# Second attention: a half head's row sums are turned and stored behind the transposes of its probabilities

## The chip, the cores and the metric

The kernel runs on one core of a Trainium2 chip, as one launch. The metric is the device time of that launch in microseconds (us), the median of several runs. In the profile PE is the matrix engine (PEld its weight loads), DVE the vector engine, ACT the scalar engine, POOL GpSimd, and SP the engine whose queue issues all the DMAs spoken of here.

## The reference

Two layers of an encoder over a prompt of 1024 rows and 8 samples of 16 rows each. Layer 0 has a sliding window with learned sinks; layer 1, the second attention, has chunk-band attention with a bias by clipped distance and no sinks. Cut to what matters here:

```python
s = einsum('bqkgd,bskd->bkgqs', q, k) * ATTN_SCALE + bias
s = where(valid, s, NEG_INF)          # own chunk of 64 and 8 before it
p = softmax(s, axis=-1)               # layer 1: no sinks
o = einsum('bkgqs,bskd->bqkgd', p, v) # 16 heads of 64
x = layer_norm(ALPHA * x + (1 + gate) * (o @ w_o))
```

The kernel doesn't divide the probabilities by their row sums. It multiplies exp(s - m) with the values, and multiplies the result by one over the row sum afterwards. All products are in float32 quality: each operand is split into a high and a low part, and products are summed from them.

## The kernel before

The program is written as one list of calls. A planner then lays the instructions out: it simulates the list, gives each engine a fixed order, and takes among the instructions that it holds to be ready the one that was called earliest. So the place of a call is a rank and not a slot, and each engine then runs its fixed order on the chip and waits where data isn't there.

`attention(l, wk)` runs once for each layer (`l` 0 and 1). The queries of layer 1 are handled as 16 heads (`c` 0 to 7, `a` 0 and 1), each head in two halves of 512 queries (`h` 0 and 1), each half in two pairs of query tiles of 128. `work` holds the 64 pairs and `halves` the 32 halves. The loop over pairs does the following for pair `i`, with `k = i // 2`:

- `scores(x)`: matmuls of scores for two query tiles (lines 558 and 561), and `softmax`: bias and row minimum on DVE (line 525), the exponential with its row sum on ACT (line 529). The row sums go to columns of `L`.
- On every second pair, `sums(halves[k - 1])`: DVE takes one over the 4 columns of row sums of the half that has just been scored (line 633), PE turns them into rows (line 635), DVE copies them out of their PSUM bank to `rl` (line 636), and SP stores them to `rD` in DRAM (line 638).
- By the table `QAT`, the load of a query weight (`qload`) or a third of a head pair's queries (`qblock`, 24 matmuls at line 313, with ACT and DVE at lines 511 and 512).
- On every second pair, `weigh(halves[k - 1])`: PE transposes the half's probabilities in blocks of 128 x 128 (line 587), four to a group and PSUM bank; ACT casts a group to its high part (line 593), and DVE subtracts to get the low part (line 594). A first half (`h` 0) has 10 blocks in 3 groups, a second half 20 blocks in 5.
- With a lag of two pairs, `finish`: `values` multiplies the transposed probabilities with the values (line 609, out by lines 622 and 623), and `normalise` loads the stored row of 1/sum from `rD`, spread over 64 partitions, into `rb` (line 644, SP), multiplies by it on POOL (line 647; the last half on DVE), and stores the result to `oN` (line 649) for `c` under 6 or splits it into the operand of the out-projection. After a second half come the loads of the next head's keys and values (`kload`, lines 488 and 489).
- Behind these, one or more steps of the 16 sample items (lines 683 to 762), which have their own loads (line 689: cached values `cvB`), transposes (727, 749) and matmuls (701, 736). Eight begin from pair 24 on and eight from pair 51 on.

PSUM banks are handed out when the call is made. For transposes there is a ring, `tbk`, which in layer 1 has the three banks 4, 5 and 6 (`TB[1]`). `sums` takes one bank of it, `weigh` one for each group, and a sample item two. Whoever gets a bank waits until it has been emptied by those who had it three takings before.

The last half's `sums` and `weigh` are called behind the loop, in this order.

## Time and profile before

| | |
|---|---|
| runs | 2728.51, 2730.09, 2737.56 us; median 2730.09 |
| profiled execution | 2731.29 us, of which the span is 2729.5 us |
| mean granted PE clock | 0.986 |
| second attention | about 1530 to 1870 us of the span |

A view of the profile is read as follows. A row of the windows view gives start and end of a stretch, its length, then busy us of PE, PEld, DVE, ACT and POOL with their instructions in brackets, the granted PE clock, the busy share of the DMA engines, and GB/s. A row of the waits gives who waited, for whom, the us in total, how often, and the longest. A row of the timeline gives the start in us, the duration in us, the engine, the line, the operation, tiles written and read, the count, and in square brackets how long the engine had been idle and what ended it. A row of the groups gives the line, engine, operation, tiles and shapes, the count, then busy us and the mean ns of one, and last the idle time before them with what ended most of it.

### The profile page before, as it was taken

How to read it: one execution, taken by the hardware profiler on the slowest of the kernel's cores; microseconds unless marked ns; L12 is line 12 of the kernel's file. 1: busy time of each engine (PE TensorE's matmuls, PEld its weight loads, DVE VectorE, ACT ScalarE, POOL GpSimd, SP SyncE). 2: the span in 40 equal slices, each digit the busy share in tenths (PEclk: the TensorE clock that was granted, in tenths of full speed). 3: DMA queues.
4: the chain of work that ended last, by engine and by line, in shares of the span. 5: the costliest groups of instructions: out<-in, count | busy, mean ns of one | idle time of the engine just before them, and what ended most of it. 6: DMA issues, size and time to landing. Idle time of an engine off the chain costs nothing.

```text
span 2729.5 us, 47042 instructions
## 1 busy us (share of the span) xinstructions
PE 2633.3 (96%) x17266; PEld 2342.5 (86%) x17266; DVE 1928.2 (71%) x3840; ACT 1347.8 (49%) x2777; POOL 1069.9 (39%) x771
## 2 busy tenths in 40 slices
PE   7999889999999999999999999989999999999997
PEld 5997768989999998787898888867899999998786
DVE  4376767876677675757764677776878776878668
ACT  3476733543343344444446666672445554546553
POOL 3132523444344347675220121242467666552101
PEclk8999999999999999999999999989999999999999
DMA  8756434644444447666658457784445334349673
GB/s 295 225 158 200 156 104 173 220 172 139 149 150 138 153 138 242 216 227 218 239 191 277 147 151 194 201 243 138 162 149 185 139 126 146 116 145 306 214 237 124
DMA packets 229527, 498.27 MB, mean 183 GB/s; under 512 B 37456, under 2 KB 99232, under 8 KB 229296
## 3 DMA queue, kind: packets, MB, share of 16 engines
q1 hardware_dynamic: 229296, 495.27, 55.0%
q8 instruction: 136, 2.23, 0.3%
q14 instruction: 95, 0.78, 0.1%
HBM read 378.15 MB, written 126.47 MB: 185 GB/s over the span
## 4 chain that ended last, share of the span: by engine, by line
PE 40%; DVE 5%; DMA 2%; ACT 1%; issue 1%; POOL 1%; SPq 0%; DVEq 0%; ACTq 0%; POOLq 0%
PE PS L1237 18%; PE PS L1627 7%; PE PS L326 5%; PE PS L313 4%; PE PS L609 2%; PE PS L587 2%; PE PS L558 1%; PE PS L561 1%; PE PS L736 0%; DMA xa<-actD 0%; DVE F L525 0%; DVE wl L194 0%; DVE xa L194 0%; DMA F<-in_cvB_dram 0%; PE PS L1043 0%
## 5 line engine op out<-in xcount | busy, mean ns | idle before, releaser
L1237 PE MATMUL PS<-H,wh 128*128 128x256 f32 (+1 forms) x2304 | 353.5, 295 | 0.0
L1237 PEld LDWEIGHTS PS<-H,wh 128*128 128x128 f32 x2304 | 320.7, 189 | 0.0
L1197 DVE TENSOR_TENSOR F<-PS,F 128x256 f32<-128x256 f32 (+1 forms) x446 | 197.1, 451 | 162.2 <-PE PS L1237 155.3
L183 ACT CAST wh<-F 128x512 fp32r<-128x512 f32 (+3 forms) x221 | 135.5, 624 | 198.5 <-PE PS L1237 93.8
L194 DVE TENSOR_TENSOR wl<-F,wh 128x512 fp32r<-128x512 f32 (+2 forms) x205 | 193.7, 956 | 45.4 <-ACT wh L183 43.7
L1237 PE MATMUL PS<-H,wl 128*128 128x320 f32 (+1 forms) x1152 | 201.5, 296 | 4.9 <-ACT F L1204 2.5
L1237 PE MATMUL PS<-xa,wh 128*128 128x320 f32 (+1 forms) x1168 | 178.9, 294 | 0.0
L1237 PEld LDWEIGHTS PS<-H,wl 128*128 128x128 f32 x1152 | 169.2, 189 | 10.7 <-issue 4.1
L647 POOL TENSOR_TENSOR F<-F,x2r 64x512 f32<-64x512 f32 x62 | 79.2, 1278 | 213.8 <-DVE F L623 202.0
L1237 PEld LDWEIGHTS PS<-xa,wh 128*128 128x128 f32 x1168 | 162.2, 188 | 0.0
L1495 DVE TENSOR_TENSOR xa<-xa 128x384 fp32r<-128x384 f32 x66 | 100.3, 1531 | 80.2 <-ACT xa L183 78.3
L183 ACT CAST wh<-ws 128x512 fp32r<-128x512 f32 (+1 forms) x123 | 90.8, 745 | 115.8 <-PE PS L1237 51.3
L1357 POOL TENSOR_TENSOR F<-F 128x1152 f32<-128x1152 f32 x44 | 124.7, 2833 | 44.2 <-DVE F L1350 25.1
L313 PE MATMUL PS<-H,w0r 128*128 128x384 f32 (+1 forms) x720 | 137.5, 341 | 0.1
L1286 DVE SCALAR_TENSOR_TENSOR F<-F 128x1024 f32<-128x1024 f32 (+2 forms) x160 | 132.4, 876 | 5.0 <-ACT F L1325 4.1
L326 PE MATMUL PS<-xa,H 128*128 128x512 f32 x504 | 131.0, 401 | 5.0 <-ACT xa L183 3.3
L525 DVE CUSTOM_DVE_ANT_0 F<-PS,F,C 128x256 f32<-128x256 f32 (+3 forms) x208 | 97.2, 479 | 51.6 <-PE PS L561 25.0
L313 PE MATMUL PS<-H,wh 128*128 128x384 f32 (+1 forms) x672 | 132.7, 339 | 0.0
L313 PEld LDWEIGHTS PS<-H,w0r 128*128 128x128 f32 x720 | 125.1, 189 | 1.8 <-DVE F L525 0.4
L587 PE MATMUL PS<-C,F 128*128 128x128 f32 x720 | 112.3, 280 | 7.0 <-DVE C L636 3.1
L326 PEld LDWEIGHTS PS<-xa,H 128*128 128x128 f32 x504 | 95.1, 192 | 27.5 <-ACT xa L183 3.8
L326 PE MATMUL PS<-wh,H 128*128 128x512 f32 (+1 forms) x468 | 117.4, 359 | 0.7 <-ACT wh L183 0.5
(361 smaller groups left out, 6937.7 us busy)
## 6 DMA issues: line engine op xcount, KB each, us to landing
ws<-in_adaw_dram SPq DMA_DIRECT2D x63, 512.0 KB
ws<-in_wup_dram SPq DMA_DIRECT2D x51, 512.0 KB
F<-in_adaw_dram SPq DMA_DIRECT2D x49, 512.0 KB
actD<-F SPq DMA_DIRECT2D x33, 576.0 KB
F<-in_wup_dram SPq DMA_DIRECT2D x37, 512.0 KB
ws<-in_wdn_dram SPq DMA_DIRECT2D x33, 512.0 KB
F<-in_wdn_dram SPq DMA_DIRECT2D x33, 512.0 KB
xa<-kH SPq DMA_DIRECT2D x60, 256.0 KB
```

The source lines that it names most:

```text
L183: nc.scalar.copy(out, in_)
L194: self.eng(el).tensor_sub(lo, src, hi.bitcast(F32))
L313: mm = self.nc.tensor.matmul(out[:, 0:n], w[a][:, k * 128 : k * 128 + 128], H[:, p, k, s0 : s0 + n], start=i == 0, stop=i == 23)
L326: self.nc.tensor.matmul(out[:, 0:n], H[:, p, j * kn + k, t0 : t0 + 128], w[a][:, k * n : k * n + n], start=i == 0, stop=i == 23,)
L525: nc.vector.tensor_tensor_reduce(out=p[:, c0 : c0 + w], in0=ps, in1=b, scale=1.0, scalar=init, op0=ALU.add, op1=ALU.min, accum_out=nm)
L587: nc.tensor.transpose(t[:, n * 128 : n * 128 + 128], p[:, (kt - k0) * 128 : (kt - k0) * 128 + 128], self.ident)
L1197: nc.vector.tensor_add(d, v(ps), a if len(a.shape) == 3 else v(a))
L1237: self.pairmm = nc.tensor.matmul(ps[:, 0:m], w[a][:, k * 128 : k * 128 + 128], x(p, k, n), start=start and c == 0, stop=c == 11, skip_grou ...
L1286: nc.vector.scalar_tensor_tensor(o, u, cw[:, cc, i : i + 1], o, op0=ALU.mult, op1=ALU.add)
L1357: nc.gpsimd.tensor_mul(yg, yg, ya)
L1495: nc.vector.tensor_sub(lo, raw, hi.bitcast(F32))
L1627: self.downmm = nc.tensor.matmul(ps, a[p][:, i * 128 : i * 128 + 128], w[q], start=first and c == 0, stop=last and c == 2, skip_group_chec ...
```

## The change

In layer 1 alone, a half's `sums` is called behind its `weigh`; in layer 0 it stays where it was. The two calls behind the loop, for the last half, are not changed.

```diff
             scores(x)
             k = i // 2
-            if i % 2 == 0 and k:
+            if i % 2 == 0 and k and l == 0:
                 sums(halves[k - 1])
             for c, bi in QAT.get(i, ()) if l == 0 or i > 1 else ():
...
                     qblock(c, bi, qw[c])
             if i % 2 == 0 and k:
                 weigh(halves[k - 1])
+                if l:
+                    sums(halves[k - 1])
             if i > lag and (i - lag) % 2:
                 finish((i - lag) // 2)
```

The order in which `tbk` hands out banks changes with it: for two halves of a head it was sums, 3 groups, sums, 5 groups, and it becomes 3 groups, sums, 5 groups, sums.

## The prediction

> **What bounds the kernel now.** I read the page's head and busy rows first, to see which engine sets the time, then the windows over the second attention (1530 to 1870 us, the stretch in which lines 626 to 638 run with `l == 1`), then PE's waits in it.

> ```profile
> span 2729.5 us, 47042 instructions
> PE 2633.3 (96%) x17266; PEld 2342.5 (86%) x17266; DVE 1928.2 (71%) x3840; ACT 1347.8 (49%) x2777; POOL 1069.9 (39%) x771
> 1700.00:1790.80 90.80, 87.22 (x650) 76.19 (x648) 65.21 (x204) 60.49 (x140) 23.01 (x19) 1.00 0.76 218
> 1790.80:1797.60 6.80, 6.72 (x41) 5.17 (x42) 5.28 (x22) 5.51 (x12) 2.66 (x3) 0.50 0.99 298
> 1797.60:1811.30 13.70, 11.40 (x102) 8.50 (x101) 9.14 (x35) 10.51 (x25) 12.71 (x7) 1.00 0.81 214
> 1811.30:1818.10 6.80, 5.17 (x43) 3.48 (x44) 2.75 (x8) 1.10 (x3) 2.43 (x5) 0.50 0.94 302
> sum 340.00, PE 323.84 PEld 278.17 DVE 242.88 ACT 222.75 POOL 85.81; mean PE 46.26 PEld 39.74 DVE 34.70 ACT 31.82 POOL 12.26
> ```

> PE is busy 96% of the whole span, and 323.84 of these 340 us. So PE bounds the stage, and a change that leaves PE's instructions as they are can win no more than its 16.2 us of idle time there, plus what the two short stretches with a granted clock of 0.50 cost. The waits say who owns the idle time:

> ```profile
> PE PS L736 <- DMA F<-in_cvB_dram: 3.9, 1, 3.9
> PE PS L587 <- DVE C L636: 3.1, 5, 0.9
> PE PS L558 <- DVE C L525: 2.4, 6, 0.7
> PE PS L727 <- DVE wh L594: 1.0, 1, 1.0
> ...
> PE PS L587 <- DVE wh L594: 0.5, 1, 0.5
> ...
> PE PS L587 <- DVE x2r L594: 0.3, 1, 0.3
> ```

> The second row is what the change is aimed at: five times, 3.1 us in all, a transpose of probabilities (line 587) stood on PE until VectorE had copied the turned row sums out of their PSUM bank (line 636). That is 0.11% of the span. One of the five, in order of time:

> ```profile
> 1558.90 0.18 DVE L633 RECIPROCAL F<-F 128x4 f32<-128x4 f32 x1 [0.26 <-ACT F L529]
> 1558.93 0.44 PE L587 MATMUL PS<-C,F 128*128 128x128 f32 x2
> 1559.20 0.27 PE L635 MATMUL PS<-C,F 128*4 128x128 f32 x1
> ...
> 1559.86 0.28 DVE L636 COPY C<-PS 4x128 f32<-4x128 f32 x1
> 1560.07 0.67 DVE L594 TENSOR_TENSOR wh<-PS,wh 128x512 fp32r<-128x512 f32 x1
> 1560.19 1.25 PE L587 MATMUL PS<-C,F 128*128 128x128 f32 x8 [0.72 <-DVE C L636]
> ...
> 1560.79 0.42 PEld L587 LDWEIGHTS PS<-C,F 128*128 128x128 f32 x4 [0.18 <-DVE wh L594]
> ```

> The ring of three banks (`TB[1]`) explains it. The sums take a bank, groups 1 and 2 of the half take the other two, and group 3 needs the sums' bank back. PE had run groups 1 and 2 and the sums, and stood 0.72 us until the copy had ended. Note the last row: group 4, the next in line, takes group 1's bank, and its weight loads already waited for group 1's subtraction (line 594). That row decides how much of the wait can be won.

> **The change part by part.** `sums` of a half is called behind `weigh` of the same half instead of ahead of it, and so also behind the query block (`qblock`) or weight load (`qload`) that some pairs have in between. It applies to halves 0 to 30 of the second attention; the last one, called behind the loop, stays as it is. Nothing is added or removed: per half one reciprocal, one PE transpose, one copy and one store change their place, here with what they cost:

> ```profile
> L635 PE MATMUL PS<-C,F 128*4 128x128 f32 x32 | 8.8, 276 | 0.0
> L636 DVE COPY C<-PS 4x128 f32<-4x128 f32 x32 | 8.8, 276 | 5.8 <-PE PS L635 5.3
> L633 DVE RECIPROCAL F<-F 128x4 f32<-128x4 f32 x31 | 5.3, 171 | 7.4 <-ACT F L529 7.3
> L647 POOL TENSOR_TENSOR F<-F,x2r 64x512 f32<-64x512 f32 x31 | 39.6, 1278 | 111.4 <-DVE F L623 104.3 <-DMA x2r<-rD 5.7 <-ACT C L529 0.8
> ```

> (1) *The wait that goes.* In the new order the bank ahead of a half's first group is that of the previous half's sums, copied out long before. So "L587 <- DVE C L636" goes: 3.1 us at the most. But what is late next is group 4, on line 594. In the stretch above, without the copy on VectorE the subtraction would begin at 1559.86 or so in place of 1560.07, and group 4 would begin earlier by no more than the copy's 0.28 us; group 3 only moves into the hole and the rest of the 0.72 us shows as a wait for line 594. Five times 0.276 us gives **1.4 us won**; the bounds are 0 (the planner fills the holes differently) and 3.1.

> (2) *The wait that comes.* The sums' transpose now takes the bank of the group two before the half's last, and must wait until ScalarE's cast and VectorE's subtraction have emptied it. Before, this transpose never stood (0.0 idle in its row). Nothing shows it in its new place; the nearest rows are groups 4 and 5 of the second halves of a head, which wait for just such an evacuation: 0.5 and 0.3 us in all over 32 groups (two in each of 16 halves). Thirty-one sums at that rate: **0.8 us lost**. Bounds: 0, when PE has other work planned in between, and 31 times the longest wait of any transpose for line 594 (1.0 us), 31 us. I take 0.8, since the rows on the same banks stand so near to it. Queued behind the waiting transpose on PE are the next pair's scores (line 558) and query blocks (line 313), and behind those VectorE's line 525 and ScalarE's exponentials.

> (3) *VectorE.* Reciprocal and copy, 0.45 us a half, go behind three or five subtractions. The sum is the same; VectorE is busy 242.88 of 340 us, so the order matters only where PE waits for it, which (1) and (2) hold. Cost 0; without that cover it would be 31 x 0.45 = 14 us.

> (4) *Store, load and product.* The store (line 638), its load back (line 644) and the multiplication (line 647) come later by the length of a half's transposes, some 3 us (1559.20 to 1562.35 above, where the last group of the half starts at 1561.75 and runs 0.60), and by up to a query block more on those pairs that have one. On POOL that is hidden: of the 111.4 us before its 31 products, 104.3 were ended by the values (line 623) and only 5.7 by the load. POOL is busy 85.81 of 340 us and PE waits for none of these products. Cost 0. On SP's queue the cover is thinner; that is the second rival.

> (5) *The end of the stage.* The last half keeps its order, so what out-projection waits for at the end is unchanged: 0.

> Sum: -1.4 + 0.8 = **-0.6 us** on the profiled execution's own 2731.29 us (span 2729.5 and 1.8 around it): 2730.7. The median of the three runs is 2730.09, 1.2 lower, which gives 2729.5.

> **The rivals.**

> *All of it is won, and the clock with it.* The static order is planned anew for the whole stage; if work falls into the hole behind group 3, all 3.1 us go. The two stretches at clock 0.50 (1790.80 and 1811.30) both follow upon idle time on PE; their 6.72 and 5.17 us of PE work would take half as long at 1.00. If one of them goes, 2.6 to 3.4 us more, so -6.2 us: 2724. For it: one of the five waits (0.37 us at 1785.36) is among the stalls just ahead of 1790.80. Against: the wait ahead of 1811.30 is a load's (3.9 us for `cvB`), which the change doesn't touch. Chance 0.14.

> *SP's queue stands longer (slower).* SP issues in order, and already stands behind the sums:

> ```profile
> SPq L644 <- DMA rD<-C: 51.0, 23, 4.4
> SPq L638 <- DVE C L636: 37.3, 18, 11.4
> ...
> 1787.66 0.27 SPq L638 DMA_DIRECT2D rD<-C  x1
> ...
> 1792.81 0.45 SPq L644 DMA_DIRECT2D x2r<-rD  x1
> 1793.36 0.53 SPq L689 DMA_DIRECT2D F<-in_cvB_dram  x1
> ```

> Here the load of the cached values went out right behind line 644, which had waited for the store. In the late part of the stage (from pair 51) eight sample items each need such a load, DMA is nearly full (0.99 and 0.94 in the windows above), and PE has already stood 3.9 us for one. If stores that land 3 us later hold four of these eight loads back by 3 us each, 12 us are lost: 2742. It decides from three loads on (9 us, over 0.3%). Against: fifteen of sixteen such loads cost PE nothing now, and the planner issues the later store later, with other loads ahead of it. Chance 0.16, with the dearer outcomes of (2) in it.

> *The order hardly changes.* Before, the sums already ran between groups 2 and 3, not ahead of group 1: the planner places by readiness, not by the calls' order alone. If it puts them there again, the time stays at 2730. Chance 0.08.

> [...] So hardly: chance 0.02. [...]

> **How the numbers follow.** About 0.3% (8.2 us) is what a measurement of this kernel can tell from no change; the three runs before already lie 9 us apart. Forecast, no change: chance 0.60, 2729.5, within about 4 us. All won: 0.14 at 2724, of which 0.04 passes 8.2 us (both slow-clock stretches gone: 3.1 + 5.9 = 9.0 us). SP's queue or PE at the sums: 0.16 at 2742, of which 0.05 stays below 8.2 us. Order unchanged: 0.08 at 2730. Clock: 0.02. So faster 0.04, slower 0.11 + 0.02 = 0.13, same 0.83. The range runs from 2723 (just past the second case) to 2738 (through those slower cases that lose two or three loads); outside are some 0.05 below and 0.13 above.

> **What would show it.** (1) right: no wait of line 587 for line 636, and more time of line 587 waiting for line 594; wrong if PE's idle time in the stage falls by 3 us or more. (2) right: line 635 with about 1 us idle before it, ended by line 594; wrong at 5 us or more. (4) right: POOL's waits for `rD` grow from 5.7 us with no new wait on PE; wrong if PE's waits for `in_cvB`, `kH` or the biases grow by over 3 us, which is the slower rival. PE's idle time in the stage staying between 14 and 18 us is the forecast; a granted clock of 0.50 elsewhere in the stage would shift it either way. What would make all of it wrong is an order of the stage planned so differently that stalls appear in places which none of these rows names.

## The result, and the profile after

| | before | after |
|---|---|---|
| runs | 12 | 12 |
| median, us | 2732.72 | 2739.05 |
| lowest to highest, us | 2728.47 to 2739.35 | 2736.74 to 2745.60 |
| ratio | | 1.0027, 95% interval 1.0017 to 1.0036 |
| profiled execution, us (span) | 2731.29 (2729.5) | 2741.53 (2739.7) |

The changed kernel is slower by 0.27%, about 7 us. That is under the 0.3% that the prediction took as the least that can be told from no change, yet the interval excludes no change, and 2739.05 us lies 1 us above the forecast range, which ended at 2738. Here and below, ratios and intervals leave out three disturbed executions at a mean clock of 0.60 to 0.67 (3582.78 us of g0, 3965.15 of m1 and one of the kernel before), while the medians are of all executions. The twelve runs of the kernel before have a median 2.6 us higher than the three that were known at the prediction, so part of the miss is the base; the rest is the change.

Where does it lie? The planner's order on PE, DVE and ACT is the same in both kernels up to the second attention and again behind its end, as the order of the instructions in the two traces shows. So the change can act only within the stage itself, counted here from the first score matmul of layer 1 to the end of its last product with values (line 609). Three profiles exist of each order with all transfers done and on SP's queue: among the experiments below, e3 and e5 keep the order of the kernel before on these engines, and e1 and k1 that of the changed one (k1 but for a few instructions). From the fourth column on, the figures are us:

| profile of | order | ratio to before | stage, us | PE idle in it | clock at 0.50 in it | PE's waits for `cvB` |
|---|---|---|---|---|---|---|
| before | old | 1 | 351.8 | 17.7 | 13.7 | 3.9 |
| e3, four row buffers | old | 1.0004 | 350.4 | 19.0 | 6.8 | 4.9 |
| e5, store late | old | 0.9992 | 349.5 | 18.4 | 6.8 | 5.3 |
| after | new | 1.0027 | 355.5 | 19.6 | 17.1 | 6.3 |
| e1, four row buffers | new | 1.0026 | 359.5 | 26.2 | 17.1 | 13.6 |
| k1, early sums | new | 1.0033 | 357.4 | 22.1 | 17.1 | 8.6 |

The stage takes 350.6 us on the mean in the old order and 357.5 in the new one: 6.9 us, the whole of the difference in time, and no profile of one order lies among those of the other. (The stretches ahead of the stage and behind it differ by 1.5 and 0.3 us on the mean, the other way.) Of the 6.9 us, 4.3 are more idle time of PE (18.4 to 22.6), and the waits for the sample items' cached values alone grow by 4.8 (4.7 to 9.5). The clock stands at 0.50 for 8.0 us more (9.1 to 17.1), in which PE loses, by an estimate, up to half, 4.0 us (in the kernel before, the 24 matmuls of a sample item's product take 0.99 us at 1740.2, where the clock is 1.00, and 1.66 us at 1812.9, where it is 0.50); what is left of the 6.9 us, 2.6, fits in that.

The page's head after:

```profile
span 2739.7 us, 47040 instructions
PE 2638.6 (96%) x17266; PEld 2344.9 (86%) x17266; DVE 1933.0 (71%) x3840; ACT 1345.3 (49%) x2777; POOL 1066.4 (39%) x771
```

PE is as much the bound as before. Its waits in the stage (who waited, for whom, us in total, times, longest):

```profile
PE PS L736 <- DMA F<-in_cvB_dram: 6.3, 2, 4.3
PE PS L558 <- DVE C L525: 2.7, 5, 0.8
PE PS L587 <- DVE C L636: 2.5, 2, 1.3
...
PE PS L587 <- DVE x2r L594: 0.7, 1, 0.7
...
PE PS L587 <- DVE wh L594: 0.2, 1, 0.2
```

The wait that was to go, line 587 for line 636, is still there: 2.5 us in two waits where it was 3.1 in five. The waits for line 594 are 0.9 us, as they were (0.8). The first row has grown, and in the other two profiles of this order it has grown more.

Next, the four instructions that were moved and the product that hangs on them. The groups by form, over the stage of the changed kernel, then POOL's waits, then SP's:

```profile
L635 PE MATMUL PS<-C,F 128*4 128x128 f32 x32 | 8.8, 276 | 0.3 <-DVE C L758 0.2
L636 DVE COPY C<-PS 4x128 f32<-4x128 f32 x32 | 8.8, 274 | 14.0 <-PE PS L635 9.5 <-DMA rD<-C 4.4
```

```profile
POOL F L647 <- DMA x2r<-rD: 82.0, 15, 12.5
POOL F L647 <- DVE F L623: 27.8, 6, 9.1
```

```profile
SPq L644 <- DMA rD<-C: 57.3, 27, 4.7
SPq L649 <- POOL F L647: 48.1, 18, 4.6
```

PE hardly stands at the sums' transpose (0.3 us over 32). But POOL's products, which waited 5.7 us for the loaded sums before and 104.3 for the values, now wait 82.0 for the sums and 27.8 for the values. The cover has turned round. And SP, which issues in order, stands 48.1 us in front of the store of the product (line 649) where it stood 23.5.

Two ordinary means say how late the sums are. From a half's reciprocal (line 633) to its transpose (635) it takes 2.5 us on the mean of 32 halves before and 7.6 after; to its store (638) 3.8 and 10.3; to the load back (644) 7.4 and 13.7.

What SP's queue makes of it is seen at the seventh sample item. First the kernel before, SP's timeline, then the changed kernel:

```profile
1729.57 0.37 SPq L689 DMA_DIRECT2D F<-in_cvB_dram  x1
1730.23 0.27 SPq L638 DMA_DIRECT2D rD<-C  x1
1730.60 0.47 SPq L649 DMA_DIRECT2D oN<-F  x1
1731.16 1.08 SPq L691 DMA_DIRECT2D F<-vS  x1
1732.33 0.45 SPq L488 DMA_DIRECT2D xa<-kH  x1
```

```profile
1737.44 0.47 SPq L649 DMA_DIRECT2D oN<-F  x1
1738.01 1.17 SPq L488 DMA_DIRECT2D xa<-kH  x2
1739.27 0.54 SPq L689 DMA_DIRECT2D F<-in_cvB_dram  x1
...
1745.64 0.99 PE L736 MATMUL PS<-F,C 128*32 128x128 f32 x24 [2.03 <-DMA F<-in_cvB_dram]
```

Before, the load of the values went out ahead of the product's store and of the next head's keys, 10.6 us before its matmuls began (1740.2), and PE didn't wait. After, it stands behind a store that had to wait for the late product, and behind two loads of keys of 256 KB each; it goes out 6.4 us ahead of its matmuls, and PE stands 2.03 us.

But the queue is only a part of it. The items' values have a single buffer, so a load can't go before PE has ended the product (line 736) of the item before. These are PE's rows of the sixth and the seventh item, first before, then after:

```profile
1728.87 1.00 PE L736 MATMUL PS<-F,C 128*32 128x128 f32 x24
...
1740.17 0.99 PE L736 MATMUL PS<-F,C 128*32 128x128 f32 x24
```

```profile
1736.69 0.99 PE L736 MATMUL PS<-F,C 128*32 128x128 f32 x24
...
1745.64 0.99 PE L736 MATMUL PS<-F,C 128*32 128x128 f32 x24 [2.03 <-DMA F<-in_cvB_dram]
```

Before, PE had 10.3 us of other work between the two products; after, it has 5.9 us (8.0 less the 2.03 that it stood). That time is called the room ahead of the product below. The load took 6.2 us from its issue until PE was released, so even if it had been issued at once it would have come no sooner than PE did. The six profiles of the table agree. In the old order (before, e3, e5) the seventh load goes out as soon as the buffer is free, the room is 10.3 us, and PE doesn't wait. In the new order (after, e1, k1) the load goes out 1.6, 6.9 and 2.8 us behind the freeing of the buffer, the room is 5.9 us, and PE waits 2.03, 8.72 and 3.24 us. This one item makes up nearly all of the 4.8 us in the table. At the eleventh item PE waits as long in both orders: 3.85, 4.88 and 5.35 us in the old one, 4.31, 4.89 and 4.64 in the new one.

VectorE, too, meets the late store. `rl` is one buffer, and the copy of the next half may not overwrite it until the store has read it (timeline of the changed kernel, rows of one place):

```profile
1719.48 0.43 SPq L638 DMA_DIRECT2D rD<-C  x1
...
1720.84 0.27 PE L635 MATMUL PS<-C,F 128*4 128x128 f32 x1
...
1725.08 0.28 DVE L636 COPY C<-PS 4x128 f32<-4x128 f32 x1 [3.01 <-DMA rD<-C]
...
1725.41 0.33 PE L587 MATMUL PS<-C,F 128*128 128x128 f32 x1 [1.17 <-DVE C L636]
...
1726.59 0.58 PE L558 MATMUL PS<-xa 128*128 128x320 f32 x1 [0.85 <-DVE C L525]
```

The copied row of the half before (copy ended at 1714.56) was stored only at 1719.48, behind loads of values, keys and biases. The next copy stood 3.01 us for it, with everything behind it on VectorE, and PE stood 1.17 and 0.85 us. That is the wait of line 587 for line 636, come back by another way.

### The profile page after: what moved, and what is told of

The parts are those of the page before. It is cut to its first block, busy times and chain, and to the rows that moved or that the text cites. A ratio compares the mean times of both kernels' runs of the same rounds, so it can differ in the third digit from the quotient of the medians.

```text
span 2739.7 us, 47040 instructions
## 1 busy us (share of the span) xinstructions
PE 2638.6 (96%) x17266; PEld 2344.9 (86%) x17266; DVE 1933.0 (71%) x3840; ACT 1345.3 (49%) x2777; POOL 1066.4 (39%) x771
## 4 chain that ended last, share of the span: by engine, by line
PE 33%; DVE 6%; DMA 5%; ACT 3%; issue 2%; POOL 1%; SPq 1%; DVEq 0%; POOLq 0%; ACTq 0%
PE PS L1239 14%; PE PS L1629 6%; PE PS L313 4%; PE PS L326 4%; PE PS L609 2%; PE PS L587 1%; DVE wl L194 1%; DMA F<-hmD 1%; PE PS L558 1%; PE PS L561 1%; ACT F L940 1%; DMA rD<-C 0%; DMA F<-in_cvB_dram 0%; PE PS L736 0%; DMA xa<-actS 0%
## 5 line engine op out<-in xcount | busy, mean ns | idle before, releaser
L194 DVE TENSOR_TENSOR wl<-F,wh 128x512 fp32r<-128x512 f32 (+2 forms) x205 | 200.8, 990 | 43.2 <-ACT wh L183 40.9
L647 POOL TENSOR_TENSOR F<-F,x2r 64x512 f32<-64x512 f32 x62 | 80.6, 1300 | 231.3 <-DVE F L623 124.4
L525 DVE CUSTOM_DVE_ANT_0 F<-PS,F,C 128x256 f32<-128x256 f32 (+3 forms) x208 | 97.2, 479 | 43.5 <-PE PS L561 20.7
L587 PE MATMUL PS<-C,F 128*128 128x128 f32 x720 | 113.2, 281 | 5.9 <-DVE C L636 2.5
```

The lines of the kernel that those rows point to most:

```text
L194: self.eng(el).tensor_sub(lo, src, hi.bitcast(F32))
L525: nc.vector.tensor_tensor_reduce(out=p[:, c0 : c0 + w], in0=ps, in1=b, scale=1.0, scalar=init, op0=ALU.add, op1=ALU.min, accum_out=nm)
L587: nc.tensor.transpose(t[:, n * 128 : n * 128 + 128], p[:, (kt - k0) * 128 : (kt - k0) * 128 + 128], self.ident)
```

## The experiments

Five theories, as the expectations name them. **A**: the single row buffer `rl`, as just shown. **B**: the late sums make the product late, SP stands for it, and sample loads come late. **C**: any edit makes the planner find another order, and times differ by some 5 us without a cause. **D**: the loss is spread over many small waits. **E**: the ring of banks, not the place of the call, makes the sums late. Every run is compared with runs of the kernel before on the same chip. Line numbers in a profile of an edited kernel are higher by up to 5 behind the edit.

### e1 and e3: four row buffers, in the new and in the old order

```diff
-        rl = sc.take(128)
+        rt = sc.take(128)
+        rls = Ring([rt[o : o + 4] for o in ((0, 32, 64, 96) if l else (0,))])
...
-            nc.vector.tensor_copy(rl[0:4, :], t[0:4, 0:128])
+            rl = rls.next()
+            nc.vector.tensor_copy(rl, t[0:4, 0:128])
```

> The changed kernel, with four row buffers (partitions 0, 32, 64, 96 of rl) in place of one in the second attention. Theory A (single row buffer): in the changed kernel VectorE stood 4.4 us, in two pieces, at line 636 until the late store of the half before had read rl, and PE stood 2.5 us for that copy and some more behind it; without it the time falls by 2 to 5 us against the changed kernel, to about 2735, and 'DVE C L636 <- DMA rD' is gone. Theory B (late product: SP stands for the product at line 649, 48.1 us against 23.5, and sample loads come late, 6.3 us against 3.9): no change, about 2739, the waits for in_cvB stay. Theory C (the stage is planned anew, and any edit gives another time within some 5 us): anything from 2730 to 2742, with stalls in other places.

> The kernel before, with the same four row buffers: the control for e1. Theory A: no wait of that kind stood in this stage before, so 2732 within 2 us. Theory B: the same. Theory C: off by up to 5 us either way although nothing that waited is taken away.

Measured: e1 2740.73 us, ratio 1.0026 (1.0014 to 1.0037); e3 2733.82 us, 1.0004 (0.9991 to 1.0017). The planner's order on PE, DVE, ACT and POOL is that of the kernel without the edit in both, so this takes a wait away and nothing else. In e1's profile VectorE no longer stands for the store, and line 587 waits 0.4 us for the copy in place of 2.5. The time stays. PE's waits in e1, where line 738 is the items' product with values:

```profile
PE PS L738 <- DMA F<-in_cvB_dram: 13.6, 2, 8.7
PE PS L559 <- DVE C L526: 1.9, 4, 0.7
...
PE PS L738 <- DVE F L624: 1.7, 2, 1.3
```

Theory A falls as the cause: what was won at the copy, PE stood for at the load of values, 8.72 of the 13.6 us at the seventh item.

### e4: behind the query block, but ahead of weigh

```diff
-            if i % 2 == 0 and k:
+            if i % 2 == 0 and k and l == 0:
                 sums(halves[k - 1])
...
             if i % 2 == 0 and k:
+                if l:
+                    sums(halves[k - 1])
                 weigh(halves[k - 1])
```

> Half of the move: sums behind the query block, but still ahead of weigh. Theories A and B: the sums are late only on the pairs with a query block or load, and the ring of banks is that of before, so between the two kernels, 2733 to 2736, with 'L587 <- DVE C L636' as before (some 3 us). Theory C: anything from 2728 to 2742.

Measured: 2731.67 us, ratio 0.9999 (0.9986 to 1.0013), under the 2733 to 2736 that theories A and B were given. The sums are as early as before (transpose 2.5 us behind the reciprocal), and line 587 waits 3.1 us for line 636 as before. So moving past the query block costs nothing; what costs is moving past `weigh`. The order does differ from the kernel before in places, and the time doesn't: a point against theory C.

### e5: the store alone behind weigh

```diff
+            if l == 0 or x.c * 4 + x.a * 2 + x.h == 31:
+                rstore(x, rl)
+
+        def rstore(x, rl):
+            hh = 2 * x.c + x.a
             q0 = x.h * 512
             nc.sync.dma_start(self.rD[l][hh, q0 : q0 + 512].rearrange("(g q) -> g q", q=128), rl[0:4, :])
...
                 weigh(halves[k - 1])
+                if l:
+                    rstore(halves[k - 1], rl)
```

> Reciprocal, transpose and copy where they were before, the store to rD alone called behind weigh. Theory B in the form that the store's rank alone makes it late: slower than before, about 2737, with POOL's waits for rD up from 5.7 towards 82 us. If lateness comes from the transpose's rank (in the changed kernel the transpose follows the reciprocal by 1 to 16 us, before by 0 to 9): about 2732, POOL's waits for rD stay under 20 us. Theory C: off by up to 5 us either way.

Measured: 2731.51 us, ratio 0.9992 (0.998 to 1.0005). The order came out as in the kernel before on every engine, SP's queue included: a lower rank of the store moves nothing. The second of the two expected cases holds: lateness comes with the transpose. As the order is unchanged, this run also shows how far two measurements of one program lie apart here, 0.08%.

### g1 and g0: without the loads of cached values

```diff
-                nc.sync.dma_start(v3, I["cvB"][s, :, 512 * p : 512 * p + 512].rearrange("(k p) d -> p k d", p=128))
+                if (p, s) == (0, 0):
+                    nc.sync.dma_start(v3, I["cvB"][s, :, 512 * p : 512 * p + 512].rearrange("(k p) d -> p k d", p=128))
```

> The changed kernel without 15 of the 16 loads of cached values in the second attention (the first item's values serve all), so that no sample item can wait for one. Theory B (the late sums hold SP's queue, and loads of cached values come too late for PE): the difference to the same edit of the kernel before (next run) shrinks from 6 or 7 us to under 2 us. Theory D (the loss is spread: more standing at the sums' bank, at scores and casts, as PE's other waits): 4 to 7 us of difference remain. Both kernels should be faster than with the loads.

> The kernel before with the same 15 loads of cached values left out: the partner of the run above. PE's wait for in_cvB (3.9 us in the profile of before) goes: 2726 to 2730. With theory B the run above lies within 2 us of this one, with theory D 4 to 7 us above it.

Measured: the new order 2730.01 us, ratio 0.9987 (0.9973 to 1.0001); the old order 2734.97 us, 1.0007 (0.9998 to 1.0015). On PE, DVE and ACT each has the order of its kernel with the loads. So the same order of PE's work that loses 0.27% with these loads is ahead of the old one by 0.20% without them (the two intervals overlap by 0.03%), and its stage takes 346.5 us against 352.3 in the one profile that there is of each. That goes further than either theory had expected: not only is the loss gone, the sign has turned. The expectation that both would be faster was wrong for the old order; there the wait moved on to the small load of new values, 3.4 us. PE's waits in g1:

```profile
PE PS L737 <- DMA F<-vS: 2.5, 1, 2.5
PE PS L558 <- DVE C L525: 1.9, 4, 0.7
```

A caution: 15 loads of 512 KB less also leave the DMA engines 7.9 of 498 MB less to move, in a stretch where they have little room (busy share 0.76 to 0.99 in the windows of the prediction, 0.98 from 1739.3 to 1745.5 us of the changed kernel). The room ahead of the seventh product is the same 5.9 and 10.3 us in these two profiles, but there is no load to wait for. So these runs say that the loss hangs on the loads; whether SP's queue or the shorter room is why, they don't say.

### h1 and h0: the store of the results issued by POOL

```diff
-                nc.sync.dma_start(self.oN[c, r, q], on[r, q])
+                (nc.gpsimd if l else nc.sync).dma_start(self.oN[c, r, q], on[r, q])
```

> The changed kernel with the store of the results to oN (line 649) issued by POOL, behind its own product, in place of SP, which stood 48.1 us for that product (before: 23.5). Theory B, with this store as what holds the loads: the loads of cached values are issued earlier and the time falls to 2731 to 2735. If SP's standing at the load back of the sums (line 644, 57.3 against 51.0 us) is what holds them, or theory D: no change, 2738 to 2742. Issuing by POOL may cost some time of its own.

> The kernel before with the store of the results to oN issued by POOL: the control for the same edit of the changed kernel, which brought 1.0010 against 1.0027. Theory B: here SP stood only 23.5 us for the product and PE's loads were hardly late, so 2730 to 2733 (ratio 0.999 to 1.001). If the edit is worth 4 or 5 us whatever the order, 2727 to 2729, and it says nothing about the change.

Measured: new order 2735.59 us, ratio 1.0010 (0.9996 to 1.0024); old order 2733.02 us, 1.0016 (1.0001 to 1.0030). The order on PE, DVE and ACT is again untouched in both. The edit costs the old order 0.16% and wins the new one 0.17%, and between the two nothing is left of the loss (0.06% the other way, within the intervals). Both came out above what theory B had given them, h1 by 0.6 us and h0 by 0.0006 of its ratio, and h1's interval overlaps that of the changed kernel (1.0017 to 1.0036). What the edit takes away is SP's standing for the product, and it is worth something only where the product is late. That fits theory B, but doesn't show it alone: in h1's profile PE's waits for the loads are 5.8 us, hardly less than the 6.3 of the changed kernel:

```profile
PE PS L736 <- DMA F<-in_cvB_dram: 5.8, 2, 3.3
...
PE PS L587 <- DVE C L636: 1.6, 1, 1.6
```

The seventh load goes out at 1733.93, 0.4 us behind the freeing of its buffer, and PE, which comes to the product after 5.9 us, still stands 2.47 us for it. SP's queue is out of the way there; what remains is the shorter room against the 7.9 us that the load took from its issue until PE was released.

### j1: the load back issued by POOL as well

```diff
-            st = nc.sync.dma_start(rb[r, :], bass.AP(src.tensor, src.offset, [[0, 64], [1, 512]]))
+            st = (nc.gpsimd if l else nc.sync).dma_start(rb[r, :], bass.AP(src.tensor, src.offset, [[0, 64], [1, 512]]))
```

> The changed kernel with both the load back of the sums (line 644) and the store of the results (line 649) issued by POOL, so that SP stands for neither the sums' landing nor the product. Theory B: sample loads go out earlier than in the run with the store alone moved; 2728 to 2734. If what is left against before is not SP's standing, 2735 to 2738 as with the store alone.

Measured: 2734.92 us, ratio 1.0010 (0.9995 to 1.0026), the same as h1. The order on PE, DVE and ACT is another one here, so the two don't differ in the queue alone: the room ahead of the seventh product is 7.4 us, and PE doesn't wait there. SP's standing at the load back is not what remains, or POOL's own standing (46.2 us for the stored sums) eats what is won; this run doesn't tell these two apart.

### k1 and m1: why the sums are late

```diff
                 if l:
-                    sums(halves[k - 1])
+                    with self.tc.high_priority():
+                        sums(halves[k - 1])
```

> The changed kernel with the sums' instructions given a higher rank in the plan: the order of the banks is the new one, but reciprocal, transpose, copy and store come as soon as they are ready. Theory B: the lateness is gone, POOL's waits for rD fall from 82 to under 20 us, and the wait of line 587 for line 636 (3.1 us before) goes too: 2729 to 2733, and perhaps a little faster than before. Theory D with the new order of banks as the cause: still slower, 2736 to 2741.

Measured: 2740.76 us, ratio 1.0033 (1.0020 to 1.0046). Asking for a higher rank left the plan nearly as it was: transpose 7.6 us behind the reciprocal, as in the changed kernel, and only a few instructions near 1740 us change places. The run is in effect a repeat of the changed kernel.

```diff
-            t = self.bank(tbk.next())
+            t = self.bank((sbk if l else tbk).next())
             nc.tensor.transpose(t[0:4, 0:128], L[:, cs], self.ident)
```

> The changed kernel with the sums' transpose taking its bank from the scores' ring of four in place of the ring of three that the groups use. Theory E (the ring, not the rank of the call, makes the sums late: the bank two groups back has to be emptied first): the transpose follows the reciprocal by under 4 us on the mean (changed kernel 7.6, before 2.5), POOL's waits for rD fall from 82 to under 30 us, and the time falls to 2728 to 2735. If rank makes them late: still some 7 us, and 2737 to 2741.

> The kernel before with the sums' bank from the scores' ring, called at the old place. The wait of line 587 for line 636 (3.1 us) must go, since no group shares a bank with the sums any more. If that wait is worth what it lasts: 2729 to 2730. If the next group's wait for its own bank takes its place, as the prediction had it: 2731 to 2733. A worse ring for the scores would show as more waits of line 558.

Measured: m1 (called at the new place) 2747.10 us, 1.0056 (1.0035 to 1.0077); m0 (at the old place) 2749.59 us, 1.0069 (1.0046 to 1.0092). Theory E's first half holds: with a bank from the scores' ring the transpose follows the reciprocal by 2.6 us on the mean although `sums` is called behind `weigh`. It is the bank that makes the sums late, not the place of the call. With the groups' ring, the sums behind `weigh` have to wait until the bank of the group two before the last has been filled, cast and subtracted. POOL's waits for the sums fall from 82.0 to 42.5 us, not to under 30. The time that was expected of it doesn't come: both kernels are slower than before. Their stages take 355.2 and 359.3 us (old order 350.6 on the mean), and behind the stage it takes 867.4 and 869.2 us to the last instruction, against 856 to 861 in the six profiles of the table. So these runs don't show what early sums would win. One stall of 4.9 us in the out-projection belongs to the loss behind the stage, in PE's waits of m1:

```profile
PE PS L587 <- ACT F L529: 5.8, 11, 2.1
PE PS L326 <- DVE F L1124: 4.9, 1, 4.9
```

In m0 line 587's wait for line 636 is gone, as it had to be, and its waits for line 594 grow from 0.8 to 5.4 us: the next group's wait does take its place there. The scores (line 558) now wait 5.2 us for the copy, a wait that no row of the kernel before shows. Why the plan is worse behind the stage was not followed up. Here theory C has its place: an edit to the bank ring can move the plan by more than the effect under study.

### r1, r0, r2: the items' values loaded by POOL

```diff
-                nc.sync.dma_start(v3, I["cvB"][s, :, 512 * p : 512 * p + 512].rearrange("(k p) d -> p k d", p=128))
+                nc.gpsimd.dma_start(v3, I["cvB"][s, :, 512 * p : 512 * p + 512].rearrange("(k p) d -> p k d", p=128))
...
-                nc.sync.dma_start(vn, vS[16 * s : 16 * s + 16, 512 * p : 512 * p + 512])
+                nc.gpsimd.dma_start(vn, vS[16 * s : 16 * s + 16, 512 * p : 512 * p + 512])
```

> The changed kernel with the sample items' loads of cached and new values (lines 689 and 691) issued by POOL in place of SP; all loads are done. If SP's queue holds these loads: PE's waits for in_cvB fall from 6 to 14 us in the profiles of the new order to under 4, and the time to 2728 to 2734. If the single buffer of values or the DMA engines hold them: no change, 2737 to 2742. POOL's own standing ahead of the loads may cost a few us of it.

> The kernel before with the same loads issued by POOL, the partner of the run above. SP's queue theory: 2729 to 2734, within 2 us of the run above or above it. Otherwise some 6 us under it.

> As the first of these runs, with the four row buffers added, so that VectorE doesn't stand for the store of the half before (4.4 us in the profile of the changed kernel). If both the loads and the copy are out of the way, the new order is the faster one: 2726 to 2730, ratio 0.997 to 0.999. If the loads stay late: 2737 to 2742.

Measured: r1 2736.69 us, 1.0021 (1.0011 to 1.0031); r0 2734.70 us, 1.0010 (1.0000 to 1.0021); r2 2737.79 us, 1.0017 (1.0006 to 1.0028). The difference between the two orders shrinks from 0.27% to 0.11%, but the intervals overlap, and none of the three beats the kernel before. r1 lies between its two cases, r0 0.7 us above its first, and r2, which was to be the fastest, in its second. The order on PE, DVE and ACT changes with this edit, so the runs don't differ from their partners in the queue alone. POOL's waits in r1:

```profile
POOL F L647 <- DMA x2r<-rD: 47.6, 11, 9.7
...
POOL F L689 <- PE PS L736: 19.1, 6, 10.6
```

POOL is the very engine whose products wait for the late sums (first row), and now it also stands 19.1 us at the loads until their buffer is free (second row). In r1 the seventh load goes out 0.1 us behind the freeing of its buffer and PE waits 0.3 us there; of its 4.2 us for `cvB`, 3.9 are at the eleventh item, whose load goes out 3.8 us behind the freeing of its buffer, after other work of POOL (line 194) and a product. In r0 PE waits 1.0 us for `cvB`, in r2 8.9. So the wait at the seventh item can be nearly taken away, and r1 is still 0.21% behind the kernel before.

No version with all its work beat the kernel before; e5 and e4 can't be told from it.

## Why the prediction was wrong, point by point

- **What bounds the kernel**: right. PE is busy 96% of the span in both, and the loss shows up as PE's idle time (4.3 us more) and as a lower clock in the stage (8.0 us more at 0.50).
- **(1) The wait that goes, 1.4 us won of 3.1**: wrong in this kernel, though the reasoning on the banks was sound. The wait for the sums' bank came back through the single row buffer (2.5 us in two waits), which the part didn't look at. With that taken away (e1) it is 0.4 us, and it was worth nothing, since PE stood for a load instead. That line 594 would take its place didn't happen in the changed kernel (0.9 us against 0.8), but it did in m0, where the calls stand as before and no group shares a bank with the sums (5.4 us).
- **(2) The wait that comes, 0.8 us**: wrong in kind. The bank was the right thing to look at, but it was priced as PE standing at the transpose. PE stood 0.3 us. The planner knows the wait and gives PE other work, so the price is paid in lateness: 5.1 us more between reciprocal and transpose, shown by m1 to come from the bank.
- **(3) VectorE, cost 0**: nearly right. It stood 4.4 us for the late store, which no row of before showed, and taking that away changed nothing.
- **(4) Store, load and product, cost 0**: this is the step that failed. It had the lateness at some 3 us, the length of the transposes, and its price at nothing; the lateness was some 6.5 us to the store (3.8 to 10.3), because the bank's evacuation comes on top. At that size the cover on POOL, 104.3 us of waiting for values, is gone: POOL waited 82.0 us for the sums. The step noted that the cover on SP's queue was thinner, and left it to a rival. With the items' loads done the new order loses 0.27%, without them (g1 and g0) it loses nothing.
- **(5) The end of the stage**: right, nothing there.
- **The second rival, SP's queue stands longer, 2742 us at a chance of 0.16**: this came nearest, at a chance of 0.16, and by a mechanism that is its own only in part. Right was that loads of cached values come late behind SP's queue and that PE stands for them, 4.8 us more on the mean of three profiles each. Wrong was which: it named four of the eight late items, but the late eleventh costs the same in both orders, and the growth is at the seventh, one of the early eight. Wrong was also the transfer that holds SP up: it spoke of the load back of the sums (57.3 against 51.0 us), and what grew most was the wait for the product at its store (48.1 against 23.5). And it had nothing of the other part: PE's new order leaves 5.9 us in place of 10.3 between the sixth product and the seventh. That belongs to the prediction's last sentence, an order planned so differently that stalls appear where no row names them.
- **The clock**: the forecast had it as a gain if all went well. It was a loss, in stretches behind PE's idle time: 8.0 us more at 0.50 on the mean.
- **Order unchanged** (0.08) and **Clock: 0.02**: neither. The order changed within the stage. The term of 0.02, a clock that falls where transposes stand closer together, is shown by no run: in the changed kernel 16 of the 24 matmuls from 1634.6 to 1638.0 us are transposes of line 587, and the clock was 1.00 there and up to 1726.7. The stretches at 0.50 follow upon stalls (see below).

What stays open: how much of the loss is SP's lateness and how much the shorter room that the new plan leaves ahead of the seventh product, with a single buffer of values and DMA engines that were busy at 0.98 while the seventh load was under way. A run with two buffers of values, in both orders, would let the loads go ahead of that room, and none was made. Nor is it shown why the plans of m0 and m1 lose some 10 us behind the stage.

## What to carry to other kernels

When instructions are moved behind others that share a ring of buffers, ask not only whether an engine will stand for the buffer but how much later the result comes: here the planner hid the wait (PE stood 0.3 us) and passed on the delay (5.1 us). Follow that delay to the next queue that works in order: here SP stood 48.1 us in place of 23.5 for the late products, with other transfers behind, and the one that hurt, a load of values for which PE stood 2.03 us, belonged to other work altogether. Look also at how much other work the new plan leaves between the freeing of a buffer and its next use, since a load that was early enough before may not be so now (5.9 us of room in place of 10.3). A wait of 3 us seen on the bounding engine isn't worth 3 us until it is known what that engine would do next (in e1 the wait fell from 2.5 us to 0.4, and the time stayed).

## What the runs showed of the hardware

```profile
1791.40:1794.80 3.40, 1.59 (x8) 0.88 (x7) 2.02 (x9) 2.51 (x5) 0.98 (x1) 1.00 1.04 375
1815.40:1818.80 3.40, 0.21 (x2) 0.00 (x0) 2.06 (x6) 1.95 (x5) 3.40 (x2) 1.00 1.05 316
1723.30:1726.70 3.40, 1.38 (x14) 0.61 (x13) 1.56 (x5) 0.61 (x2) 0.00 (x0) 1.00 1.05 259
1743.80:1747.20 3.40, 1.56 (x29) 1.19 (x30) 1.56 (x6) 0.48 (x2) 0.00 (x0) 0.99 0.83 201
```

PE's busy time is the second number: 1.59, 0.21, 1.38 and 1.56 us of 3.4, so three of these four windows were busy for 41 to 47%. Idle time of 1.8 to 2.0 us in all stood ahead of three of these falls. By an estimate, 3.4 us at 0.50 cost PE up to 1.7 us more: the 24 matmuls of an item's product (line 736) took 0.99 us at 1745.64, where the clock was 1.00, and 1.66 us at 1819.92, where it was 0.50. That less idle time would do is not shown: in the kernel before, a stretch of the same length with 2.05 us of PE's work (1522.6 to 1526.0) had no fall behind it.
